# Loads moved in a one-core decoder block: the background convolution's inputs and the branches' outputs

## The chip, the cores and the metric

The kernel runs on one core of a Trainium2 chip. The metric is the device time of one execution in microseconds; the median of three runs stands for the kernel.

## The reference

One layer on a sequence of 2048 tokens and 1024 features, all in float32:

```python
xn = rmsnorm(h, g_mix)
z = xn @ w_in + b_in                      # 1024 -> 1536: a, gate, p of 512 each
u = a * sigmoid(gate)
v = causal_depthwise_conv(u, w_dw) + b_dw # 31 taps, 512 channels
y_conv = silu(layernorm(v, ln_g, ln_b))
y_pool = per group of 128 channels: (trailing mean over 2, 4, 8 or 16 tokens - token) @ w_pool, times s_pool
h = h + concat(y_conv, y_pool) @ w_out
h = h + (silu(n @ w_gate) * (n @ w_up)) @ w_down   # n = rmsnorm(h, g_ffn); 1024 -> 2816 -> 1024
out = rmsnorm(h, g_final)
```

## The kernel before, in words

The sequence is cut into two halves of 1024 tokens, `a0` and `a1` (class `Sup`). Features lie on the partitions, tokens along the free dimension. Every float32 product is made of three matmuls (`mm3`, L204 to L208): both operands are split into a high part, cast by ScalarE (L197), and a low part, subtracted by VectorE (L198); `split` does both. The gate, up and down products use Strassen's seven products of half-size blocks: a `Quad` is one 256-row block of the result, with seven products of twelve matmuls and evacuations on ScalarE and VectorE (L933 to L980). Down products are made in three groups of the hidden dimension; the first two are `DownQuad`s (eight in all), the third is the plain loop `down` (L770).

Order of the work around the change, for `a0`: twenty-two gate/up quads (numbers 0 to 21) and eight down quads (22 to 29) in one generator, `gate_up` (L654); then the last down group, `down` (L770), of eight tiles with 36 matmuls each; then `a1`'s output projection and its own quads. The factors of the down products are loaded from DRAM and split by `factors` (L745): the first set while quad 21 runs, the second while quad 25 runs.

Beside the quads of `a0` runs, on VectorE, the background generator of `a1`: four pools (L443), then `mix_branches` (L576), which is the convolution of the four channel groups (L477) and the layer norm (L532). `beside` (L1048) advances it by six steps for every seven of the quads. A channel group's convolution is one multiply-add per tap: L492 for tap 0 and L494 for the 30 others, into a buffer v, from a buffer u of 1054 columns. For `a1`, u was stored to DRAM early (L424) and is loaded back by SP (L481) at the group's start, followed by a step of its own. The four v stay until the layer norm is over; its results go to DRAM (L563), as the pools' did (L463).

`down` takes, per tile, a weight block made ahead by `Ahead` (L250: one tile ahead) through `Dense` (L210: load L227, split), an h block loaded and stored every second tile (L780, L789), the evacuation L785, and a sum of squares (L312, L313). Between its tiles stand `y_load` (L467), which brings the eight outputs of `a1`'s branches back from DRAM (L472) and splits them for the output projection, and `mix_weights` (L587), which starts to load that projection's weights.

Buffers come from two arenas whose places are fixed when the program is built. `arena` has 17 units of 1056 columns. `Arena.take` (L64) picks, among free units, the one given back longest ago; a new user waits on the chip for the last one's reads and writes. In the later phase (`arena.tidy`), pairs (weight staging `st`, factor loads, h, `at`, `tx`) take even places, and single buffers (u, v, the temporary `s` of a quad, y loads, squares) take the last five units if one of them is free and any other if not:

```python
            where = (range(0, size, 2), range(size)) if n == 2 else (range(size - 5, size), range(size))
```

The framework plans the order of instructions on each engine and of the transfers on SP when it builds the program: what is written earlier goes first among what its plan has ready, so later work can be placed ahead of its step. On the chip each engine then goes through its list in order.

Of the kernel before, what the change touches and what calls it, by code (L numbers as in the profile page):

```python
# [18 lines left out]
TT = 2 * T  # L19
# [3 lines left out]
CW = 31  # L23
HALO = CW - 1
CC = 512
NCI = CC // P
# [78 lines left out]
def block_kernel(ctx: ExitStack, tc: tile.TileContext, x, xt, wi, wo, wop, wg, wu, wd, wp, par, out):  # L105
    nc = tc.nc
# [31 lines left out]
    arena = Arena(const.tile([P, N32 * G32], F32, name="arena"), G32, N32)  # L138
# [4 lines left out]
    def dram(name, n, w):  # L143
        return [dr.tile([P, w], F32, name=f"{name}{i}", bufs=1) for i in range(n)]

    u_d = dram("u_d", NCI, HALO + TT)
# [7 lines left out]
    def col(o, i=0):  # L154
        return par_sb[:, o + i : o + i + 1]
# [199 lines left out]
    class Sup:  # L355
# [111 lines left out]
        def y_load(self, qs):  # L467
            for q in qs:
                self.y[q] = r = R("y")
                for k in range(2):  # L470
# [3 lines left out]
                    t.free()  # L474
                    yield

        def conv(self, i, first=False):  # L477

            if self.s:
                u = Buf(arena, HALO + TT)  # L480
                nc.sync.dma_start(u.ap, u_d[i])  # L481
                yield
            else:
                u = self.us.pop(i)
            n = T if first else TT
            vb = self.vpe if first else B2("v")
            v = vb.ap[:, :n]
            self.vs.append(vb)
            for j in range(CW):
                w = col(O_WDW, i * CW + j)  # L490
                if j == 0:
                    nc.vector.tensor_scalar(v, u.ap[:, :n], w, col(O_BDW, i), op0=ALU.mult, op1=ALU.add)  # L492
                else:
                    stt(out=v, in0=u.ap[:, j : j + n], scalar=w, in1=v, op0=ALU.mult, op1=ALU.add)  # L494
                if j == CW - 1:
                    u.free()
                yield

        def conv_pe(self, i):
# [535 lines left out]
    def run(*gens):  # L1035
        for g in gens:
            for _ in g:
                pass

    def step(g, n=1):  # L1040
        for _ in range(n):
            next(g, None)
# [13 lines left out]
    a0, a1 = Sup(0), Sup(1)  # L1056
# [123 lines left out]
    run(bg)  # L1180
    run(a0.follow)
    dn = a0.down(STRASSEN)
    step(dn, 2)
    run(a1.y_load((2, 3, 0, 1)))
    step(dn, 4)
    a1.mix_weights()
    run(dn)
    g1 = a1.gate_up()
    turn(a1, g1)
    beside(g1, a0.final(), 1, 2)  # L1190
# [62 lines left out]
```

## Time and profile before

| what | us |
|---|---|
| median of 3 runs (1874.2 to 1879.09) | 1875.26 |
| the profiled execution, its own time | 1876.28 |
| its span | 1874.5 |
| TensorE busy | 1806.9 |
| VectorE busy | 1390.5 |
| ScalarE busy | 698.6 |
| mean granted TensorE clock | 0.984 of full |

All times in rows count from the start of the span. "Idle" is time in which an engine ran nothing, and the engine and buffer named beside it are what ended it. PE is TensorE, DVE is VectorE, ACT is ScalarE, SP is the engine that issues transfers. Of the 1874.5 us, the gate/up quads of `a0` with the background work end near 857, its down quads near 1024, its last down group near 1101; the rest is `a1`.

### The profile page before, as it was taken

The numbers are of one execution on the slowest core, as the hardware profiler recorded it, in microseconds if no ns is written. First come the engines' busy times: TensorE is split into PE (matmuls) and PEld (weight loads), VectorE is DVE, ScalarE is ACT, GpSimd is POOL, SyncE is SP. The second block draws the span as 40 slices with busy tenths as digits, with TensorE's granted clock in tenths as the row PEclk, the third lists the DMA queues.
The fourth block names the chain that finished last, engine by engine and source line by source line (L and its number), as shares of the span: only waits on it lengthen the run. The fifth ranks groups of instructions, "written<-read, shape, count | busy, mean of one in ns | idle before, by whom it ended". The sixth has DMA issues, their size and how long they took to land.

```text
span 1874.5 us, 19934 instructions
## 1 busy us (share of the span) xinstructions
PE 1806.9 (96%) x7803; PEld 1462.6 (78%) x7803; DVE 1390.5 (74%) x1607; ACT 698.6 (37%) x900; POOL 54.6 (3%) x41
## 2 busy tenths in 40 slices
PE   8999999998999999999989799899999999999996
PEld 6887887876888888887768688678888888787885
DVE  6989996478899898969996445875656464768645
ACT  6156124244333333343443333333333333625420
POOL 0013200000000000000000000000000000000000
PEclk9999999999999999999999899989999999999998
DMA  8263226522542224246657853144423322577532
GB/s 308 71 215 110 78 81 195 188 80 90 172 149 96 84 93 171 97 145 220 225 183 292 299 196 124 38 158 180 174 85 116 115 107 90 211 260 270 207 108 90
DMA packets 84511, 289.15 MB, mean 154 GB/s; under 512 B 7616, under 2 KB 11840, under 8 KB 71104
## 3 DMA queue, kind: packets, MB, share of 16 engines
q1 hardware_dynamic: 83120, 285.69, 42.9%
q10 hardware_dynamic: 1296, 2.19, 0.4%
q8 instruction: 61, 1.00, 0.2%
q14 instruction: 34, 0.28, 0.0%
HBM read 201.77 MB, written 86.08 MB: 154 GB/s over the span
## 4 chain that ended last, share of the span: by engine, by line
PE 81%; DVE 10%; DMA 3%; ACT 2%; issue 2%; POOL 0%; SPq 0%; POOLq 0%; DVEq 0%; ACTq 0%
PE quad L206 11%; PE quad L207 10%; PE quad L208 10%; PE chain L206 9%; PE chain L207 8%; PE chain L208 8%; DVE arena_r L198 4%; PE px L206 3%; PE px L208 3%; PE px L207 3%; PE pd L206 2%; PE pd L208 2%; PE pd L207 2%; DVE arena L494 2%; PE pa L207 1%
## 5 line engine op out<-in xcount | busy, mean ns | idle before, releaser
L197 ACT CAST arena_r<-arena 128x1024 fp32r<-128x1024 f32 (+2 forms) x431 | 414.2, 976 | 707.2 <-PE quad L207 191.8
L198 DVE TENSOR_TENSOR arena_r<-arena,arena_r 128x1024 fp32r<-128x1024 f32 (+2 forms) x431 | 480.0, 1130 | 192.2 <-ACT arena_r L197 187.0
L206 PE MATMUL quad<-arena_r 128*128 128x512 f32 x960 | 376.8, 393 | 5.4 <-DVE arena L1006 2.2
L207 PE MATMUL quad<-arena_r 128*128 128x512 f32 x960 | 375.6, 391 | 2.4 <-DVE arena_r L198 2.4
L208 PE MATMUL quad<-arena_r 128*128 128x512 f32 x960 | 375.6, 391 | 0.0
L206 PE MATMUL chain<-arena_r 128*128 128x512 f32 x720 | 289.8, 403 | 15.1 <-ACT arena L972 6.8
L494 DVE SCALAR_TENSOR_TENSOR arena<-arena,par_sb 128x1024 f32<-128x1024 f32 (+1 forms) x240 | 287.5, 1214 | 2.3
L207 PE MATMUL chain<-arena_r 128*128 128x512 f32 x720 | 283.9, 394 | 5.2 <-DVE arena_r L198 5.2
L208 PE MATMUL chain<-arena_r 128*128 128x512 f32 x720 | 283.1, 393 | 0.0
L206 PEld LDWEIGHTS quad<-arena_r 128*128 128x128 f32 x960 | 181.0, 189 | 47.9 <-DVE arena L1006 4.2
L207 PEld LDWEIGHTS quad<-arena_r 128*128 128x128 f32 x960 | 181.2, 189 | 41.1 <-DVE arena_r L198 3.6
L208 PEld LDWEIGHTS quad<-arena_r 128*128 128x128 f32 x960 | 181.2, 189 | 37.9
L206 PEld LDWEIGHTS chain<-arena_r 128*128 128x128 f32 x720 | 136.4, 189 | 63.9 <-ACT chain L967 22.3
L207 PEld LDWEIGHTS chain<-arena_r 128*128 128x128 f32 x720 | 136.9, 190 | 33.6 <-DVE arena_r L198 6.9
L208 PEld LDWEIGHTS chain<-arena_r 128*128 128x128 f32 x720 | 136.9, 190 | 29.2
L206 PE MATMUL px<-arena_r 128*128 128x512 f32 x256 | 100.0, 392 | 0.0
L208 PE MATMUL px<-arena_r 128*128 128x512 f32 x256 | 99.7, 389 | 0.0
L207 PE MATMUL px<-arena_r 128*128 128x512 f32 x256 | 99.7, 389 | 0.0
L933 DVE TENSOR_TENSOR arena<-quad,arena 128x512 f32<-128x512 f32 x88 | 60.4, 687 | 34.7 <-ACT arena L974 30.0
L206 PE MATMUL pd<-arena_r 128*128 128x512 f32 x192 | 76.7, 399 | 9.6 <-ACT arena_r L197 8.8
L208 PE MATMUL pd<-arena_r 128*128 128x512 f32 x192 | 76.0, 396 | 1.0 <-DVE arena_r L198 1.0
L207 PE MATMUL pd<-arena_r 128*128 128x512 f32 x192 | 75.7, 394 | 0.0
(142 smaller groups left out, 2027.6 us busy)
## 6 DMA issues: line engine op xcount, KB each, us to landing
arena<-t_d SPq DMA_DIRECT2D x28, 1024.0 KB, 5.4
arena<-h_d SPq DMA_DIRECT2D x28, 1024.0 KB, 6.0
arena<-in_wu SPq DMA_DIRECT2D x44, 512.0 KB, 4.4
arena<-in_wg SPq DMA_DIRECT2D x44, 512.0 KB, 4.4
h_d<-arena SPq DMA_DIRECT2D x20, 1024.0 KB, 4.5
t_d<-arena SPq DMA_DIRECT2D x16, 1024.0 KB, 4.3
arena<-in_wd SPq DMA_DIRECT2D x32, 512.0 KB, 5.9
arena<-in_x SPq DMA_DIRECT2D x12, 1024.0 KB, 7.3
```

Source lines behind the costliest of these rows:

```text
L197: nc.scalar.copy(hi, y)
L198: tt(out=lo, in0=y, in1=hi.bitcast(F32), op=ALU.subtract)
L206: nc.tensor.matmul(acc, lhsT=w[:, 0, c], rhs=hi, start=start, stop=False, **kw)
L207: nc.tensor.matmul(acc, lhsT=w[:, 0, c], rhs=lo, start=False, stop=False, **kw)
L208: nc.tensor.matmul(acc, lhsT=w[:, 1, c], rhs=hi, start=False, stop=stop, **kw)
L494: stt(out=v, in0=u.ap[:, j : j + n], scalar=w, in1=v, op0=ALU.mult, op1=ALU.add)
L933: tt(out=dst if self.gate else extra, in0=acc, in1=extra, op=ALU.add)
```

## The change

A channel group's input is loaded at tap 15 of the group before, instead of at the group's own start; only the first group still loads at its start, with its step. In the last down group of `a0`, the eight y loads, before written in one block after the second tile, are written one or two after each tile from the second on. `mix_weights` stays after the sixth tile.

```diff
+        def u_load(self, i):
+            self.us[i] = u = Buf(arena, HALO + TT)
+            nc.sync.dma_start(u.ap, u_d[i])
+
         def conv(self, i, first=False):
 
-            if self.s:
-                u = Buf(arena, HALO + TT)
-                nc.sync.dma_start(u.ap, u_d[i])
-                yield
-            else:
-                u = self.us.pop(i)
+            if i not in self.us:
+                self.u_load(i)
+                yield
+            u = self.us.pop(i)
...
                 if j == CW - 1:
                     u.free()
+                if self.s and j == CW // 2 and i + 1 < NCI:
+                    self.u_load(i + 1)
                 yield
...
     dn = a0.down(STRASSEN)
-    step(dn, 2)
-    run(a1.y_load((2, 3, 0, 1)))
-    step(dn, 4)
-    a1.mix_weights()
-    run(dn)
+    step(dn)
+    yl = a1.y_load((2, 3, 0, 1))
+    for n, _ in enumerate(dn):
+        step(yl, 2 if n in (1, 3) else 1)
+        if n == 4:
+            a1.mix_weights()
+    run(yl)
```

## Rows read from the trace of the kernel before

**Rows 1.** The page, part 1: busy time and share of the span, TensorE.

```profile
PE 1806.9 (96%) x7803; PEld 1462.6 (78%) x7803; DVE 1390.5 (74%) x1607; ACT 698.6 (37%) x900; POOL 54.6 (3%) x41
```

**Rows 2.** Windows: busy time (instructions) of each engine, granted clock, DMA share, GB/s.

```profile
core 0: us, PE busy (x) PEld busy (x) DVE busy (x) ACT busy (x) POOL busy (x), PEclk, DMA share, GB/s
596.00:626.00 30.00, 30.00 (x134) 24.67 (x133) 20.05 (x27) 10.46 (x14) 0.00 (x0) 1.00 0.20 68
...
790.00:838.00 48.00, 48.00 (x212) 39.35 (x211) 30.51 (x37) 23.35 (x31) 0.00 (x0) 1.00 0.40 143
838.00:947.00 109.00, 101.25 (x422) 80.11 (x421) 106.05 (x118) 43.48 (x52) 0.00 (x0) 0.97 0.62 211
...
1060.00:1080.00 20.00, 15.49 (x55) 12.23 (x56) 9.00 (x8) 4.81 (x6) 0.00 (x0) 0.74 0.65 242
```

**Rows 3.** Waits of TensorE, 1010 to 1110 us: total, times, longest.

```profile
PE pd L206 <- ACT arena_r L197: 8.8, 2, 7.2
```

**Rows 4.** Timeline of VectorE, last down group: start, duration, instruction, idle before it.

```profile
1029.69 1.23 DVE L785 TENSOR_TENSOR arena<-pd,arena 128x1024 f32<-128x1024 f32 x1 [2.56 <-PE pd L208]
...
1040.26 1.23 DVE L313 TENSOR_TENSOR arena<-arena 128x1024 f32<-128x1024 f32 x1 [1.19 <-ACT arena L312]
...
1046.01 1.22 DVE L785 TENSOR_TENSOR arena<-pd,arena 128x1024 f32<-128x1024 f32 x1 [3.08 <-PE pd L208]
...
1061.37 1.22 DVE L785 TENSOR_TENSOR arena<-pd,arena 128x1024 f32<-128x1024 f32 x1
...
1076.30 1.22 DVE L785 TENSOR_TENSOR arena<-pd,arena 128x1024 f32<-128x1024 f32 x1 [3.71 <-PE pd L208]
...
1084.23 1.22 DVE L785 TENSOR_TENSOR arena<-pd,arena 128x1024 f32<-128x1024 f32 x1 [4.36 <-PE pd L208]
...
1100.55 1.23 DVE L785 TENSOR_TENSOR arena<-pd,arena 128x1024 f32<-128x1024 f32 x1 [4.52 <-PE pd L208]
```

**Rows 5.** Timelines of SP, ScalarE and TensorE, last down group, one row each or two.

```profile
1042.95 0.33 SPq L227 DMA_DIRECT2D arena<-in_wd  x1
...
1046.64 0.83 ACT L197 CAST arena_r<-arena 128x768 fp32r<-128x768 f32 x1 [0.37 <-DMA arena<-in_wd]
...
1064.51 0.80 PE L206 MATMUL pd<-arena_r 128*128 128x512 f32 x1 [7.23 <-ACT arena_r L197]
```

**Rows 6.** The chain that ended last: start, duration, what.

```profile
963.02 1.72 PE mu L545 x4
...
1052.95 6.12 DMA arena<-y_d
```

**Rows 7.** Timelines of SP and VectorE: input loads and first taps, third and fourth group.

```profile
715.48 0.33 SPq L481 DMA_DIRECT2D arena<-u_d  x1
...
718.85 0.81 DVE L492 TENSOR_SCALAR arena<-arena,par_sb 128x1024 f32<-128x1024 f32 x1
...
790.22 0.33 SPq L481 DMA_DIRECT2D arena<-u_d  x1
...
838.23 0.81 DVE L492 TENSOR_SCALAR arena<-arena,par_sb 128x1024 f32<-128x1024 f32 x1
```

**Rows 8.** Timeline of SP: last at store, 3rd, 5th and 8th h store, both halves.

```profile
857.05 0.32 SPq L927 DMA_DIRECT2D at_d<-arena  x1
...
917.01 0.32 SPq L999 DMA_DIRECT2D h_d<-arena  x1
...
964.84 0.33 SPq L999 DMA_DIRECT2D h_d<-arena  x1
...
1024.06 0.32 SPq L999 DMA_DIRECT2D h_d<-arena  x1
...
1642.11 0.33 SPq L927 DMA_DIRECT2D at_d<-arena  x1
...
1696.05 0.33 SPq L999 DMA_DIRECT2D h_d<-arena  x1
...
1735.42 0.32 SPq L999 DMA_DIRECT2D h_d<-arena  x1
...
1793.40 0.33 SPq L999 DMA_DIRECT2D h_d<-arena  x1
```

## The prediction, made before the changed kernel ran

> **What bounds the kernel now.** The page comes first: TensorE is busy for 1806.9 us of a 1874.5 us span [rows 1], so a change off TensorE can win only idle time or slow-clock time of that engine, some 68 us in all. The windows say where it is. While the background convolution runs beside the gate/up quads TensorE has none to give: 30.00 of 30.00 us and 48.00 of 48.00 us [rows 2]. From 838 to 947 it is busy for 101.25 of 109 us while VectorE works for 106.05, and from 1060 to 1080 for 15.49 of 20 us at a granted clock of 0.74 [rows 2]. Only these two stretches, both before 1101 us, can pay: the end of the convolution beside the down quads (part A), and the last down group (part B).
>
> **Part B, the loads of y.** The waits of TensorE in the last down group are one line, 8.8 us for the cast of a weight tile, the longest 7.2 us [rows 3]. The eight evacuations at L785 give the whole loss. The last two tiles are 8.16 us apart (1084.23 to 1100.55 in two steps), the first and the last are 70.86 us apart, and seven steps of 8.16 us are 57.1 us: 13.7 us are lost, nearly all in two steps of 15.4 us (1046.01 to 1061.37) and 14.9 us (to 1076.30) [rows 4]. The idle before 1064.51 is 7.23 us, and the matmul that ends it lasts 0.80 us [rows 5]: this is the stretch at clock 0.74, levels 1.2 and 2.4 GHz mixed, and the 13.7 us hold its cost.
>
> Why it stalls: after the second tile the eight y loads are written in one block, ahead of the weight loads of all later tiles. They rotate through units 12 to 15 of the arena, two of which the first h tile held until its store, and all queue on SP; a y transfer takes 6.12 us [rows 6]. The fourth tile's weights are issued only at 1042.95 and cast at 1046.64 [rows 5], just as the third tile ends; the next weights are cast behind the last y splits, and so, on VectorE, is the evacuation at 1061.37.
>
> The edit moves loads, adds and removes none: 8 DMAs, 8 casts and 8 subtractions stay. In the new order one or two y loads follow each of tiles 1 to 6, so a weight load has at most two in front of it. A tile then asks of VectorE two y subtractions, a weight subtraction, an evacuation and a sum of squares, each under 1.25 us: some 6 of 8.16 us. The cover holds. The mixing weights are still called after the sixth tile, so nothing moves there. The last y load comes after the seventh tile, one tile (8.16 us) before the output projection wants it, which reads that part last.
>
> What is left over I find by following the allocator. The fourth tile's weights would be staged in unit 13, used last by the squares of the second tile, whose sum at L313 starts at 1040.26 and takes 1.23 us [rows 4]. Issue then, 3.7 us to arrive (1042.95 to 1046.64), 0.83 us for the cast [rows 5], about 1 us for the low part: 1047 us, against the third tile's end at 1046.0. That stays a wait of 1 us. The eighth tile has the same pattern: the squares of a tile end 3.7 us after its evacuation starts (for the second one step before 1046.01, at 1037.85, to 1041.5), 3.7 us to arrive and 1.8 us to split make 9.2 us against a tile of 8.16: 1 us again. With 1.2 us for waits that I cannot place, 3.2 us stay and **10.5 us** are won. Bounds: all 13.7 us, or, if the waits merely spread, nothing.
>
> The Trainium skill, "DMA: Bandwidth & Descriptors", section "Anatomy of one DMA — SWDGE (gpsimd) path", gives 2.0 us plus bytes over 436 GB/s (a fit for another queue than SP's), hence an estimate of 2.9 us for these 393 KB; the trace does not agree, its row has 3.7 us. By the page both waits would nearly vanish and the sum would be about 2 us larger; I go by the row.
>
> **Part A, the convolution.** What is removed is a wait ahead of each channel group. The third group's input is issued at 715.48 and its first operation starts at 718.85; the fourth's is issued at 790.22 but its first operation starts only at 838.23 [rows 7]. So the fourth is not held by its load. Its accumulator v got unit 8 of the arena, used just before by a factor load, and waits for that factor's splits: at that point the last five units, meant for one-unit buffers, held v0, v1, v2, the new u, and s of the running quad. The gap before the second group (596 to 626) is of this kind too. In these gaps VectorE works 20.05 of 30 us and 30.51 of 48 us [rows 2]: 10 and 17.5 us idle.
>
> With the load at the middle tap of the group before, allocation shifts. Followed by hand: u1 goes to unit 8 and v1 takes unit 14, just left by u0, so the second group follows the first at once. v2 then takes unit 15 from the s of quad 14, the same release that let the third load go at 715.48, so the third group starts only 3 us earlier: what the second won is returned as idle. v3 takes unit 12, just left by u2, with u3 loaded since quad 17's end. The fourth group starts at about 787 instead of 838, and fills the 17.5 us idle: 14 of its 31 operations at 1.25 us. Three yields fewer move the layer norm up by three steps. VectorE is not saved any work, only offered it earlier; SP gets the same four loads, each to a unit that is free, so I cost them at nothing: their cover is half a group, some 35 us (718.85 to 790.22 is a whole one).
>
> What is it worth? The second half of the sequence runs the same eight down quads with no convolution beside them [rows 8]. From the last at store to the third h store: 59.96 us here, 53.94 there. The next two quads, where the second set of factors is split: 47.83 against 39.37. The last three: 59.22 against 57.97. The layer norm's mean matmuls, 1.72 us [rows 6], belong to the middle piece and stay. Without any convolution there at most 6.0 + 8.5 - 1.7 = 12.8 us are to be had. The 17 operations left still fall in the first piece (838 to about 885): I take 1 of its 6 us. The middle piece loses them all but may get the layer norm's sums instead: 5 of 6.8 us. **6 us**, between 0 (the order of VectorE's queue stays as tight) and 12.8; no loss, since the engine's work there only falls.
>
> **Sum.** 10.5 + 6 = 16.5 us off. The profiled execution took 1876.28 us (span 1874.5 and 1.8 around it), giving 1859.8; it lies 1.0 us above the median of 1875.26, so **1859 us**.
>
> **Rivals.**
> 1. The load ahead does not advance the fourth group: v3 still lands in a pair unit, or the planned order on VectorE leaves the sums where they are. For it: before, the wait was v's, not the load's, and I followed the allocator by hand. Against: unit 12 is free by the code. Only B: 1865. Chance 0.17.
> 2. B gives little: weight loads stay late because a weight's staging buffer still comes from a y split or a sum of squares. For it: the two waits above. Against: four units rotate instead of two. A with 3 us of B: 1866. Chance 0.12.
> 3. Neither does anything: 1875. Chance 0.07.
> 4. Slower: y loads now stand ahead of every tile's weights, on SP and in ScalarE's cast queue, and every such tile pays what the two did, 15.2 - 8.16 = 7.0 us [rows 4]. Six tiles are exposed. Three lose 21 us against the 13.7 + 6 that are to be had, four lose 28: from four tiles on it is slower by over 0.3%, at 1884, and at six 1898. For it: a y transfer of 6.1 us [rows 6] is most of a tile's 8.16 us, and casts stand in one queue. Against: the two tiles fell behind four or more queued y loads, not one. Chance 0.09.
>
> **Numbers.** The forecast, both parts working, has 0.55, its own range 1849 to 1866. A measurement tells 0.3% from no change, 5.6 us here. Under 1869.6: 0.55 + 0.17 + 0.10 of rival 2 = 0.82; within 0.3%: 0.09; slower: 0.09. The low end is both upper bounds, 1876.3 - 26.5 - 1.0 = 1849, taken as 1848; the high end takes in rivals 1 and 2 and part of 3: 1872.
>
> **What would show it.** In the new profile: L785 evenly 8.2 us apart, with a little more before the fourth and eighth tile; the 7.2 us wait for the cast gone and no stretch at half clock near 1070; L492 of the fourth group near 787 and that of the third near 715; the middle pair of h stores below 43 us apart. Wrong would be: L492 of the fourth group still after 830 (A), a wait for a weight cast before most tiles (B), or new idle of TensorE between 480 and 838, where it now has none.

## The result, and the profile after

The changed kernel takes 1856.49 us, the median of four runs (1854.09 to 1857.97), against 1876.1 us before: a ratio of 0.9893 (0.9875 to 0.991), 19.6 us off. The forecast was 1859 with a range from 1848 to 1872. On time it was right. Of its two terms one was too small; the other had about the right size, but the experiments show that it named the wrong cause.

The page of the changed kernel, part 1, for [rows 1]:

```profile
PE 1799.8 (97%) x7803; PEld 1460.2 (79%) x7803; DVE 1389.7 (75%) x1607; ACT 698.9 (38%) x900; POOL 54.1 (3%) x41
```

No engine has less to do: the instruction counts are equal and VectorE's 1389.7 us are its 1390.5 of before. The span fell by 18.3 us to 1856.2 (this profiled execution took 1857.97, the longest of the four). TensorE's busy time fell by 7.1 of these, with the same matmuls and a mean granted clock of 0.988 instead of 0.984; the other 11.2 us were idle. The same windows as in [rows 2]:

```profile
596.00:626.00 30.00, 30.00 (x133) 24.45 (x132) 29.72 (x34) 10.99 (x15) 0.00 (x0) 1.00 0.12 38
...
790.00:838.00 48.00, 48.00 (x212) 39.15 (x210) 47.29 (x51) 21.10 (x28) 0.00 (x0) 1.00 0.38 124
838.00:947.00 109.00, 105.64 (x456) 85.13 (x456) 107.08 (x122) 51.96 (x62) 0.00 (x0) 1.00 0.68 251
...
1060.00:1080.00 20.00, 18.11 (x80) 14.68 (x79) 9.50 (x9) 5.91 (x6) 0.00 (x0) 1.00 0.65 231
```

VectorE's idle time in two of the gaps is filled (29.72 of 30 and 47.29 of 48 us, from 20.05 and 30.51). TensorE, which had no idle there, gains only behind them: 105.64 busy us of 109 and a granted clock of 1.00, from 101.25 and 0.97. The stretch at 0.74 clock near 1070 is gone.

Input loads and first taps, timelines of SP and VectorE, for [rows 7] (line 479 now issues the load, line 494 is tap 0):

```profile
661.86 0.33 SPq L479 DMA_DIRECT2D arena<-u_d  x1
777.09 0.43 SPq L479 DMA_DIRECT2D arena<-u_d  x1
```

```profile
717.98 0.81 DVE L494 TENSOR_SCALAR arena<-arena,par_sb 128x1024 f32<-128x1024 f32 x1
...
799.29 0.81 DVE L494 TENSOR_SCALAR arena<-arena,par_sb 128x1024 f32<-128x1024 f32 x1
```

The fourth group starts 39 us earlier (838.23 before); the third starts at 717.98 although its input was issued at 661.86, 56 us ahead of use.

The stores that divide the down quads (an `at` store sends off the gate/up results for the last down group, an `h` store ends a down quad), timeline of SP, for the first four of [rows 8]:

```profile
855.99 0.32 SPq L931 DMA_DIRECT2D at_d<-arena  x1
...
914.22 0.32 SPq L1003 DMA_DIRECT2D h_d<-arena  x1
...
960.21 0.33 SPq L1003 DMA_DIRECT2D h_d<-arena  x1
...
1016.80 0.33 SPq L1003 DMA_DIRECT2D h_d<-arena  x1
```

The three pieces take 58.2, 46.0 and 56.6 us, against 60.0, 47.8 and 59.2: 1.7, 1.8 and 2.6 us less. The middle one was to fall below 43.

The last down group, timeline of VectorE (line 789 is the evacuation), for [rows 4]:

```profile
1022.16 1.22 DVE L789 TENSOR_TENSOR arena<-pd,arena 128x1024 f32<-128x1024 f32 x1
1030.20 1.23 DVE L789 TENSOR_TENSOR arena<-pd,arena 128x1024 f32<-128x1024 f32 x1 [2.37 <-PE pd L208]
...
1054.68 1.23 DVE L789 TENSOR_TENSOR arena<-pd,arena 128x1024 f32<-128x1024 f32 x1 [1.71 <-PE pd L208]
1064.80 1.22 DVE L789 TENSOR_TENSOR arena<-pd,arena 128x1024 f32<-128x1024 f32 x1
1071.00 1.23 DVE L789 TENSOR_TENSOR arena<-pd,arena 128x1024 f32<-128x1024 f32 x1 [2.28 <-PE pd L208]
1082.26 1.23 DVE L789 TENSOR_TENSOR arena<-pd,arena 128x1024 f32<-128x1024 f32 x1 [1.39 <-PE pd L208]
```

The evacuations lie 60.1 us apart from first to last, from 70.9. The one at 1064.80 is only late on VectorE (the next is 6.2 us on), so TensorE lost time before one tile alone, the eighth. Its wait is the only one left; the kernel before had, beside the line of [rows 3], a second one in this group:

```profile
PE pd L206 <- ACT arena_r L197: 1.9, 1, 1.9
```

and before:

```profile
PE pd L208 <- DVE arena_r L198: 1.0, 1, 1.0
```

The whole difference closes with three stretches, which the table below uses. They begin at the first t store, which sends off the first gate/up results for the down quads (timeline of SP, before and then changed):

```profile
470.54 0.38 SPq L923 DMA_DIRECT2D t_d<-arena  x1
```

```profile
473.58 0.38 SPq L927 DMA_DIRECT2D t_d<-arena  x1
```

From there to the group's first evacuation, the first stretch, it is 548.6 us (473.58 to 1022.16; before 470.54 to 1029.69, 559.2), the group 60.1 (70.9), and what follows it 773.9 (773.9). That is 10.6 + 10.8 + 0. Against it stand 3.0 us that this execution lost ahead of the first t store; another execution of the same kernel reached it at 469.56, 1 us earlier than before did, so those 3 us are no part of the change.

### The profile page after: what moved, and what is told of

It reads as the page before. It is cut to its first block, busy times and chain, and to the rows that moved or that the text cites. A ratio compares the mean times of both kernels' runs of the same rounds, so it can differ in the third digit from the quotient of the medians.

```text
span 1856.2 us, 19925 instructions
## 1 busy us (share of the span) xinstructions
PE 1799.8 (97%) x7803; PEld 1460.2 (79%) x7803; DVE 1389.7 (75%) x1607; ACT 698.9 (38%) x900; POOL 54.1 (3%) x41
## 4 chain that ended last, share of the span: by engine, by line
PE 77%; DVE 10%; DMA 6%; ACT 3%; issue 2%; SPq 0%; POOL 0%; POOLq 0%; DVEq 0%; ACTq 0%
PE quad L206 10%; PE quad L207 10%; PE quad L208 10%; PE chain L206 8%; PE chain L207 8%; PE chain L208 8%; DVE arena_r L198 4%; PE px L206 2%; PE px L207 2%; PE px L208 2%; PE pd L206 2%; PE pd L208 2%; PE pd L207 2%; DVE arena L496 2%; ACT arena_r L197 1%
## 5 line engine op out<-in xcount | busy, mean ns | idle before, releaser
L206 PE MATMUL pd<-arena_r 128*128 128x512 f32 x192 | 75.0, 391 | 2.7 <-ACT arena_r L197 1.9
L208 PE MATMUL pd<-arena_r 128*128 128x512 f32 x192 | 74.7, 389 | 0.0
L207 PE MATMUL pd<-arena_r 128*128 128x512 f32 x192 | 74.7, 389 | 0.0
```

Of the source, the lines that this page charges most:

```text
L206: nc.tensor.matmul(acc, lhsT=w[:, 0, c], rhs=hi, start=start, stop=False, **kw)
L207: nc.tensor.matmul(acc, lhsT=w[:, 0, c], rhs=lo, start=False, stop=False, **kw)
L208: nc.tensor.matmul(acc, lhsT=w[:, 1, c], rhs=hi, start=False, stop=stop, **kw)
```

## The experiments

Two parts that gain 10.6 and 10.8 us in two separate stretches look like the two halves of the change. The theory was that they add: the load ahead wins the first stretch, the spread y loads the second. The rival was that one part works in both.

**e1: the load ahead alone**, the diff's first half; the y loads stay one block.

> The convolution's part alone; the y loads stay one block after the second tile. Theory (the two parts add, and the traces of before and after split the gain as 10.6 us up to the first evacuation of the last down group and 10.8 us within it): 8 to 10 us faster than before, the last down group still 70 us from its first to its last evacuation, with the 7 us wait. Rival 1 (the load ahead is worth little, the gain ahead of the last down group comes from elsewhere): under 3 us. Rival 2 (a convolution that ends earlier also starts the last down group in a better order): over 14 us, with the group's 13.7 us loss cut too.

Measured: 1854.6 us against 1877.31, ratio 0.9879 (0.9864 to 0.9894): 22.7 us faster, as much as the whole change. The theory fell. First stretch 548.1 us (from 471.60), and the group, timeline of VectorE, first and last evacuation:

```profile
1019.68 1.23 DVE L789 TENSOR_TENSOR arena<-pd,arena 128x1024 f32<-128x1024 f32 x1 [3.16 <-PE pd L208]
...
1076.81 1.22 DVE L789 TENSOR_TENSOR arena<-pd,arena 128x1024 f32<-128x1024 f32 x1 [4.52 <-PE pd L208]
```

That is 57.1 us, seven steps of 8.16: no loss at all, with the block in place. TensorE waited for nothing there. Timeline of SP, the y loads of e1, and below them the first one of the kernel before:

```profile
1005.15 4.14 SPq L472 DMA_DIRECT2D arena<-y_d  x3
...
1014.70 2.44 SPq L472 DMA_DIRECT2D arena<-y_d  x3
...
1031.45 0.33 SPq L472 DMA_DIRECT2D arena<-y_d  x1
...
1040.80 0.33 SPq L472 DMA_DIRECT2D arena<-y_d  x1
```

```profile
1027.15 0.32 SPq L472 DMA_DIRECT2D arena<-y_d  x1
```

Six of the eight are issued before the group's first evacuation; in the kernel before it is one, and the last follow after 1051.

**e2: the spread alone**, the diff's second half.

> The y loads spread, the convolution as before. Theory: 10 to 11 us faster, evacuations of the last down group 60 us from first to last, the stretch to its first evacuation as before (559 us from the second t store). Rival (the spread only pays because the convolution ended earlier and left VectorE free): under 5 us, the group over 65 us.

(The 559 us of that text run from the first t store.) Measured: 1868.19 us, ratio 0.9944 (0.9931 to 0.9956): 9.1 us faster. Timeline of VectorE:

```profile
1031.36 1.23 DVE L785 TENSOR_TENSOR arena<-pd,arena 128x1024 f32<-128x1024 f32 x1 [2.37 <-PE pd L208]
...
1092.52 1.23 DVE L785 TENSOR_TENSOR arena<-pd,arena 128x1024 f32<-128x1024 f32 x1 [1.48 <-PE pd L208]
```

The group takes 61.2 us and the first stretch 557.5; the gain is a little under the 10 to 11 us expected. So the spread by itself does cure most of the stall; only, the load ahead cures it too, and wholly. The two parts do not add: 22.7 + 9.1 would have been 31.8 us.

**e3: v ahead, u not.** The accumulator v of the next group is taken at the middle tap; its input is loaded at the group's start, as before.

```diff
...
-            vb = self.vpe if first else B2("v")
+            vb = self.vpe if first else self.va.pop(i, None) or B2("v")
...
+                if self.s and j == CW // 2 and i + 1 < NCI:
+                    self.va[i + 1] = B2("v")
```

> The kernel before, with each background group's accumulator v taken at the middle tap of the group before; its input u is still loaded at the group's own start, and y loads stay one block. Theory (the fourth group was held by the buffer that v got, not by its load): its first tap moves from 838 to about 795 and 5 to 10 us are won without any load ahead. Rival (the load is what holds it): first tap still near 838, and within 3 us of before.

Measured: 1858.77 us, ratio 0.9899 (0.9885 to 0.9912): 18.5 us faster with no load ahead. Timelines of SP and VectorE, the fourth group's input and first tap:

```profile
793.44 0.33 SPq L481 DMA_DIRECT2D arena<-u_d  x1
```

```profile
798.17 0.81 DVE L492 TENSOR_SCALAR arena<-arena,par_sb 128x1024 f32<-128x1024 f32 x1
```

The load is issued when the third group ends and the tap runs 4.7 us later. So the load's lateness cost under 5 us per group; the 48 us in which the fourth group stood still were v's. The 18.5 us are more than the 5 to 10 expected, and most are not the convolution's: the group of tiles again loses nothing (56.7 us; eight even evacuations but for the first, which is late on VectorE), which is 14.2 us, while the first stretch is 555.1 us, 4.0 less than before. The load ahead won 11.1 there with a fourth group that starts at nearly the same time (796.87), so the earlier start of that group by itself does not account for its gain. TensorE was idle in this stretch for 9.0 us (5.0 in e1, 10.3 before) and busy for 546.2 (543.0 and 548.8).

**e4: the taps left out.** The kernel before with 30 of 31 background taps removed, steps and loads kept.

```diff
-            for j in range(CW):
+            for j in range(1 if self.s else CW):
...
-                if j == CW - 1:
+                if j == (0 if self.s else CW - 1):
                     u.free()
                 yield
+                if self.s:
+                    for _ in range(CW - 1):
+                        yield
```

> The kernel before with 30 of the 31 taps of the background convolution left out (the second half's convolution output is not the reference's); loads, buffers' places and steps stay. It measures what the taps cost TensorE at most. Theory: 9 to 13 us faster than before, so that the load ahead, worth about 10, has nearly all that there is. Rival (VectorE's taps cost more than the load ahead wins, more is left): over 16 us faster. Other rival (the stalls at the down quads come from the factor splits alone): under 5 us.

Measured: 1850.56 us, ratio 0.9851 (0.9838 to 0.9865): 26.7 us faster, over the 16 of the first rival. By stretches it is 12.3 in the first (472.40 to 1019.22, 546.8 us) and 13.7 in the group (57.1 us). The load ahead has 11.1 of the first. The second is again the whole loss of the group, in which not one tap runs. The edit also gives u back after its first tap instead of its last, so buffers taken later do move, other than the expectation says, and the 12.3 us are the taps and that together.

What e1, e3 and e4 share and e2 lacks is a change of which buffers are free when the group begins. Followed through the allocator for each kernel, the first h tile of the group takes units 14 and 15 in the kernel before and in e2, and 4, 8 and 2 with their neighbours in e1, e3 and e4. Units 12 to 16 are those for single buffers; the running sum of squares holds one of them through the group, and the y loads, the weight staging and the squares turn through the other four. In the kernel before, v of the fourth group had gone to unit 8; e1 leaves it in unit 12, and the order in which units were last given back differs from there on. The new theory: not the block stalls, but the block with two of its units held until the h tile is stored. Two experiments force that place; no other line of the program changes, though buffers taken later follow.

**e5: the kernel before, the h tile moved.**

```diff
...
-                    h = B4("h")
+                    h = B4("h", (range(0, 12, 2),) if m == 0 else None)
```

> The kernel before with one buffer moved: the first h tile of the last down group takes a pair among the first twelve units of the arena instead of the pair 14 and 15; the y loads stay one block and the convolution stays as it was. Theory (the stall came from that place: two of the four units that the y block and the weights turn through were held until the h tile was stored, and in the first experiment the tile had moved to units 4 and 5): the group takes 57 to 59 us from its first to its last evacuation instead of 70.9, and the kernel is 11 to 14 us faster than before. Rival (the block stalls whenever the convolution ends late and the engines' queues are full): group still over 68 us, under 3 us gained.

Measured: 1862.77 us, ratio 0.9931 (0.9919 to 0.9944): 13.5 us faster. Timelines of VectorE and of SP, the y loads up to the first evacuation:

```profile
839.09 0.80 DVE L492 TENSOR_SCALAR arena<-arena,par_sb 128x1024 f32<-128x1024 f32 x1
...
1029.60 1.22 DVE L785 TENSOR_TENSOR arena<-pd,arena 128x1024 f32<-128x1024 f32 x1 [1.83 <-PE pd L208]
...
1086.71 1.22 DVE L785 TENSOR_TENSOR arena<-pd,arena 128x1024 f32<-128x1024 f32 x1 [3.40 <-PE pd L208]
```

```profile
1018.14 4.18 SPq L472 DMA_DIRECT2D arena<-y_d  x3
...
1025.10 3.49 SPq L472 DMA_DIRECT2D arena<-y_d  x3
```

The convolution is as late as ever (839.09), the block is in place, and the group takes 57.1 us. Six y loads now go out before the first evacuation where it was one. That fits the places: by the allocator each of the four units takes two y loads; here the squares of the second tile use one of them, before the h tile held two more.

**e6: e1's kernel, the h tile put back** to units 14 and 15.

```diff
...
-                    h = B4("h")
+                    h = B4("h", (range(14, 15),) if m == 0 else None)
```

> The first experiment's kernel (load ahead alone) with the first h tile of the last down group forced to units 14 and 15, where the kernel before had it. Theory: the stall comes back, the group takes 66 to 72 us and the kernel is 8 to 14 us slower than the load ahead alone, near 1866. Rival (the earlier end of the convolution removed the stall, not the place): the group stays near 57 us and the time near 1855.

Measured: 1864.23 us, ratio 0.9934 (0.9921 to 0.9946), 12.1 us faster than before where e1 was 22.7. Timelines of VectorE and SP, and TensorE's waits in the group:

```profile
1021.46 1.23 DVE L789 TENSOR_TENSOR arena<-pd,arena 128x1024 f32<-128x1024 f32 x1 [4.29 <-PE pd L208]
...
1046.80 1.22 DVE L789 TENSOR_TENSOR arena<-pd,arena 128x1024 f32<-128x1024 f32 x1
1065.44 1.22 DVE L789 TENSOR_TENSOR arena<-pd,arena 128x1024 f32<-128x1024 f32 x1 [3.34 <-PE pd L208]
...
1089.92 1.23 DVE L789 TENSOR_TENSOR arena<-pd,arena 128x1024 f32<-128x1024 f32 x1 [4.52 <-PE pd L208]
```

```profile
1030.87 0.33 SPq L793 DMA_DIRECT2D h_d<-arena  x1
1033.28 0.33 SPq L472 DMA_DIRECT2D arena<-y_d  x1
1034.15 0.33 SPq L227 DMA_DIRECT2D arena<-in_wd  x1
1034.85 5.63 SPq L472 DMA_DIRECT2D arena<-y_d  x3
```

```profile
PE pd L206 <- ACT arena_r L197: 8.6, 1, 8.6
```

The stall is back, 68.5 us with one wait of 8.6, though the convolution ends as early as in e1. The rows of SP show how: two y loads go out before the first evacuation (1007.84 and 1017.19), and the other six bunch up behind the store of the h tile at 1030.87. The place of that tile makes the stall and removes it.

**e7: u and v both ahead**, on the load ahead, the y loads in one block.

```diff
...
                     self.u_load(i + 1)
+                    self.va[i + 1] = B2("v")
```

> The load ahead with, beside it, the accumulator v of the next group taken at the middle tap too, and the y loads in one block. Theory (the third group still waited some 35 us for its v): its first tap moves from 716 to near 690, the fourth's to near 770, and since leaving out the taps gave only 4 us more than the load ahead, 0 to 4 us are won on it: 1851 to 1855. Rival (the two together crowd the pairs and a factor or h load waits): 1857 or more.

Measured: 1853.57 us, ratio 0.9882 (0.9868 to 0.9895), against e1's 0.9879 (0.9864 to 0.9894): the same. Timeline of VectorE, first taps of the third and fourth group:

```profile
671.65 0.81 DVE L494 TENSOR_SCALAR arena<-arena,par_sb 128x1024 f32<-128x1024 f32 x1
...
776.33 0.81 DVE L494 TENSOR_SCALAR arena<-arena,par_sb 128x1024 f32<-128x1024 f32 x1
```

The third group starts 44 us before e1's (715.66) and the fourth 21 us before (796.87), and yet the first stretch is 552.9 us (472.07 to 1024.99), 4.8 longer than e1's. TensorE is idle in it as little as in e1 (5.3 us), but busy for 547.6 us instead of 543.0, at a granted clock of 0.98 instead of 1.00 behind the last at store. That the times are equal all the same comes from what follows the group: 770.4 us where e1 has 774.7. More lead buys nothing.

**e8: the changed kernel once more**, on the chip of e5 to e7.

> The changed kernel itself, beside the others on one chip. Theory (with the load ahead the block no longer stalls, so spreading it wins nothing and its one wait of 2 us stays): 1855 to 1858, 0 to 3 us slower than the load ahead alone. Rival (spreading adds to it): faster than the load ahead alone by 3 us or more.

Measured: 1856.3 us, ratio 0.9898 (0.9883 to 0.9914). The load ahead alone, which ran on another chip, is 1.7 us below it by medians, each against its own runs of before 22.7 and 20.0 us; the intervals overlap. What can be said is that the spread adds nothing to the load ahead. Its group takes 60.0 us (1017.72 to 1077.68) where e1's takes 57.1, with the one wait of 1.6 us, so if there is a difference it is a loss.

| kernel | off the median of before, us | first stretch | group | what follows |
|---|---|---|---|---|
| before | | 559.2 | 70.9 | 773.9 |
| the change | 19.6, again 20.0 | 548.6, again 548.2 | 60.1, again 60.0 | 773.9, again 772.4 |
| e1 load ahead | 22.7 | 548.1 | 57.1 | 774.7 |
| e2 spread | 9.1 | 557.5 | 61.2 | 770.0 |
| e3 v ahead | 18.5 | 555.1 | 56.7 | 772.1 |
| e4 no taps | 26.7 | 546.8 | 57.1 | 772.5 |
| e5 h tile moved | 13.5 | 558.5 | 57.1 | 773.8 |
| e6 load ahead, h tile back | 12.1 | 549.4 | 68.5 | 773.0 |
| e7 u and v ahead | 22.7 | 552.9 | 57.1 | 770.4 |

Stretches are in us, of one profiled execution each. What follows the group has the same program lines in all and still spreads over 4.7 us, so the stretches do not add up to the medians.

## Why the prediction was right, and where it was not

**The time.** 16.5 us were forecast off the profiled execution and 19.6 came off the median. The sum was short by A's term: 6 us, measured 10.6 in the first stretch of the changed kernel and 11.1 with A alone. The parts by themselves came out otherwise: A was to win 6 us and wins 22.7, B was to win 10.5 and wins 9.1, or nothing beside A. The total came near because the group's loss was counted once, under B, and could be removed only once, here by A: that much of it is luck.

**Part A, the mechanism.** Right, and tested: that the fourth group was held by v's buffer and not by its load (e3), that after the change it follows the third at once, and that the third gains little because its v waits for a quad's s (717.98, forecast 715; before 718.85; the operation on VectorE just ahead of it is the quad's last use of s). Not shown is that the earlier start is itself what wins the first stretch: with a fourth group that starts at 798.17 e3 wins 4.0 us there, with one at 776.33 e7 wins 6.2, with one at 796.87 e1 wins 11.1. What makes the difference, other buffers that moved or the place of the layer norm, stays open. The tap that was forecast for 787 ran at 799.29, 12 us late: the third group's operations, started at about the same time, ended later than counted.

**Part A, the size.** The mis-sized term is the sum by pieces. By the stores the three pieces won 1.7, 1.8 and 2.6 us where 1, 5 and 0 were put. The sums agree, both some 6 us, but the split does not: the mean matmuls of the layer norm (1.88 us) now start at 926.90, well inside the middle piece, and no longer at its very end (963.02 before), so the middle piece, which now holds more of the layer norm, won less, and the last piece won instead. The rest of the 10.6 us, by the stores, lies ahead of the last at store (4.1: 386.5 to 382.4 us from the first t store), where the sum did not look. A store, however, only marks when VectorE got so far. TensorE's own rows (columns as in [rows 2]), ahead of and behind the last at store, before and then changed:

```profile
470.54:857.05 386.51, 384.05 (x1682) 313.55 (x1680) 343.30 (x391) 143.18 (x191) 0.00 (x0) 1.00 0.36 127
857.05:1029.69 172.64, 164.76 (x695) 130.55 (x696) 153.03 (x172) 69.39 (x82) 2.49 (x1) 0.98 0.67 235
```

```profile
473.58:855.99 382.41, 381.61 (x1672) 311.81 (x1671) 355.44 (x402) 141.06 (x189) 0.00 (x0) 1.00 0.37 127
855.99:1022.16 166.17, 162.04 (x708) 130.65 (x707) 144.13 (x164) 74.61 (x88) 1.95 (x1) 1.00 0.73 267
```

Of the 4.1 us, 1.7 are idle time that is gone (2.46 to 0.80); the rest is that the store now comes ten matmuls earlier, some 2.3 us at the 0.23 us that one takes there. Behind the store 13 more matmuls fit into 6.5 us less: idle fell from 7.88 to 4.13 us, and the busy time by 2.7 at a granted clock of 1.00 instead of 0.98. So the larger miss lies in the stretch that the sum did cover. Over the whole first stretch 5.4 us were idle time and 5.2 us were matmuls that had run slowly, a gain for which the sum had no term of its own.

The bound of 12.8 us looks confirmed by the 12.3 measured with the taps left out, but they are not the same stretch. From the last at store to the last h store of the down quads, which the bound is for, that kernel wins 5.7 by the stores; 5.3 lie ahead and 1.4 behind.

**Part B, the step that failed.** It is the sentence that the y loads "are written in one block, ahead of the weight loads of all later tiles" as the reason of the stall, with the h tile's two units named only in passing. The runs put it the other way round: the block costs nothing with four units to turn through (e5, and e1), and stalls by 11 to 14 us with the h tile in two of them (before, e6). It takes both, the block and the held units: with the h tile in 14 and 15 but the loads spread, e2 has most of the loss back. The allocator had been followed for the load ahead up to the fourth v and then for the last group as it stood before the load ahead; carried on to the group it would have shown the h tile in units 4 and 5 and the stall gone through part A. The 10.5 us for B match the 10.8 of the stretch and the 9.1 of e2, but in the changed kernel they are not B's: A alone takes 13.7 there, and B gives 3 back. One reading of rows was short too: the waits of the group were two lines, not one, with 1.0 us for a low part beside the 8.8.

**What B leaves.** Of 3.2 us that were to stay, 3.0 did (60.1 against 57.1). The first of the two waits did not come, since the unit in question was another; the second did, by the chain given, squares, then weights in the same unit. Timelines of VectorE, SP, ScalarE and TensorE, the operation ahead of the sixth tile's evacuation and the eighth tile's weights:

```profile
1063.66 1.22 DVE L198 TENSOR_TENSOR arena_r<-arena,arena_r 128x1024 fp32r<-128x1024 f32 x1 [2.65 <-ACT arena_r L197]
```

```profile
1068.75 0.33 SPq L227 DMA_DIRECT2D arena<-in_wd  x1
```

```profile
1071.97 0.83 ACT L197 CAST arena_r<-arena 128x768 fp32r<-128x768 f32 x1 [4.68 <-DMA arena<-in_wd]
```

```profile
1072.86 0.50 PE L206 MATMUL pd<-arena_r 128*128 128x512 f32 x1 [1.89 <-ACT arena_r L197]
```

They are issued 0.03 us after the sum of squares of the sixth tile ends (1067.50 and 1.22 us) and cast 3.2 us after issue, where the sum had 3.7. From the sixth evacuation to the eighth tile's first matmul it is 8.06 us (1064.80 to 1072.86), where the sum had 9.2: within a tile's 8.16. The evacuation, however, was 2.0 us late (10.12 us after the one before), because on VectorE the low part of a y load stands ahead of it and had waited 2.65 us for its cast; the second execution, e8, shows the same (3.17 us). With the evacuation on time this working leaves no wait. So what B costs here is a spread y load in the way of an evacuation, at one tile.

The Trainium skill, "DMA: Bandwidth & Descriptors", section "Anatomy of one DMA — SWDGE (gpsimd) path", led the prediction to an estimate of 2.9 us for this size, by a fit for another queue than SP's: here the trace, with 3.2 us, comes nearer to it than the row used.

**The rivals.** Rival 1 said that the wait was v's and that the load would not advance the group. The first half is true (e3); the group advanced because the load's earlier place in the program also moved v. Rival 2 (B gives little) came true in the sense that B adds nothing to A. Rival 3 (neither does anything) did not come, nor rival 4, stalls at every tile: there is one wait of 1.9 us.

## What to carry to other kernels

When buffers come from an arena in order of release, an edit that only moves a load re-deals every later buffer; follow the dealing to the end of the program, not to the edit's own use. A stall that looks like a queue filled by too many loads may be two loads waiting for a third party's store: look which instruction gave back the unit, and test it by moving that one tile. Before two parts of a change are credited with the two stretches in which time fell, run each alone.

## What the runs showed that was not expected

A block of eight 512 KB loads ahead of a group of tiles costs nothing when its buffers are free (57.1 us for seven tile steps in e1, e5 and e7, 56.7 in e3). And the group's loss in e6 is larger than its wait: 11.3 us (68.5 less 57.1) for one wait of 8.6 us; TensorE's 253 matmuls between the group's first and last evacuation kept it busy for 59.9 us, in e5 for 57.1. The window of 1040 to 1060 us of that kernel has a mean granted clock of 0.74 (part of it at the lower level of 1.2 GHz, part at 2.4), as the kernel before had after its 7.23 us of idle; the changed kernel's wait of 1.9 us is followed by no such stretch.

```profile
1040.00:1060.00 20.00, 11.42 (x41) 8.61 (x39) 12.69 (x12) 9.02 (x9) 0.00 (x0) 0.74 0.75 261
```
